# Spreading a recurrence's pieces further, moving inverses within SBUF, and reciprocal square roots by GpSimd's power

## The chip, the cores and the metric

One core of one Trainium2 chip. The metric is the device time of one execution in microseconds (us). A core has TensorE (PE, matrix products), VectorE (DVE), ScalarE (ACT), GpSimd (POOL) and SyncE (SP), which in this kernel issues all the transfers (DMAs). Each engine takes its instructions from its own queue in order; an instruction that waits holds all those behind it on its engine, and none on another.

## The reference

One layer of a streaming encoder over 4096 prompt tokens with 1024 features, and over 32 sample tokens that continue running streams with caches of their own. Group A is a short gated convolution, group B a gated delta rule with 4 heads of 128.

```python
h    = rmsnorm(x, ln_pre)
proj = h @ w_in     # columns: B_a | C_a | X_a | Z_a | qkv | Z_g | a_dec | b_beta
y_a  = b_a * conv3(c_a * x_a) * silu(z_a)
q, k, v = split(silu(conv4(qkv)));  q, k = l2norm(q), l2norm(k)
g    = -exp(a_log) * softplus(a_dec + dt_bias);  beta = sigmoid(b_beta)
S_t  = exp(g_t) (I - beta_t k_t k_t^T) S_{t-1} + beta_t k_t v_t^T;  o_t = q_t^T S_t / sqrt(dk)
y_g  = rmsnorm(o, gdn_norm_w) * silu(z_g)
y    = x + rmsnorm(concat(y_a, y_g) @ w_out, ln_post)
```

The reference evaluates the delta rule chunk by chunk: within a chunk a unit lower triangular matrix is inverted, from chunk to chunk the state S is handed on. The reciprocal square roots are those of the three norms.

## The kernel before

It runs in three stages: stage 1 (group B, and the transposed input for group A), group A, and the output products.

**Stage 1** takes the prompt in 16 blocks of 256 tokens, two chunks of 128 each; the sample's 32 tokens go with the first block. A block has eight steps (q, k, v and z, two column pairs each) of two projections, a projection being 24 products of 128x256 with weights in two float16 halves (`pj` in the profile, L74). After every projection stands a numbered slot, 16 to a block: pieces of other work are hung into the slots of their block or of the next (`at_slot`), and `run_slot` writes them out there. From block 1 on PE's order is exactly the written one: `Ordered` (T) ties each product or transpose to the one before it. The order on the other engines comes from a scheduler, which simulates the program and puts each instruction into its engine's queue by its simulated start.

The pieces of one block, in order:

- `xprep`: RMS-norm of the tokens of the next block (`xss`), with a reciprocal square root, and their transposition by DMAs; `gates` and `decays` for g and beta.
- `norm_qk` and `gram` (slots 7 to 12): normalisation and the products k k^T and q k^T (`gq` in the profile). The masked results M and `at` are kept, and the four 32x32 diagonal blocks of M of every chunk and head go through a DRAM buffer (`lad`) into the tile `la`, which holds the 32 blocks four times, 8 columns of the inverse for each copy. `rnorms` takes one square root (`r`, 128x16) for the q and k norms of the block.
- `subst`: the forward substitution, 31 steps of a multiplication and a subtraction on POOL (L551, L552), each depending on the one before. The result `lt` holds the inverses of the 32x32 blocks. It is written to DRAM (`ltd`, L555) and gathered from there by eight DMAs into `Tc` (L562), in pieces of 32 bytes.
- `merge` in five pieces: DVE transposes `Tc` into U (L583), then PE and DVE (`Rx`, L599) build the inverses of the whole chunks from the blocks, in the PSUM bank "m".
- `rec_a`, one for each chunk, in four pieces: transposed v (`rt`); k S and q S (`rk`, `rq`); U times the corrected v (`rv`), copied by ACT to `vn` (L652); and the new state (`rS`).
- `rec_b`, one for each chunk, in two pieces: the output products `at` times `vn` (`oo`), added to o by DVE, with the norm of o (`so`, 128x4, one reciprocal square root, then L682); and then the transposes of o (`om`), multiplied into `zg` by DVE (L688) and sent to DRAM by a DMA. Both pieces have their results in the PSUM bank "o", of which there is one buffer. So there is of "m".

`finish(p, s0)` hangs the merge and the recurrence of a block into slots 22 to 39 counted from the block's own first slot: that is into the second half of its own block and the first half of the next. `prep_a` prepares weights of group A besides, one in each of blocks 1 to 13 and two in 4, 7 and 10: loads (`xtw`), multiplications on DVE (L206) and POOL (L735, L741), and DMAs to `wad`.

`rsqrt` (L132) computes a reciprocal square root on DVE with eleven operations: a shift and a multiplication with an addition on the integers for a first value (L134, L135), and three rounds of Newton's method (L137 to L139).

**The transition.** After the last block, what is left in the slots (the rest of block 14, and block 15's merge and recurrence) is written out at once, the pools are closed, and group A begins (from here on the scheduler orders PE, too, and puts the rest among the first products of group A): `h_load` builds the operands `op` (for the first 512 tokens on DVE), and `winograd` makes seven products of half the size in place of eight (`pja`, `ga`).

**The output stage** multiplies by w_out (`pjo`, `go`, `ro`) and norms each half block (`norm_out`, one reciprocal square root, `oss`) before the sum is written.

Of the kernel before, what the change touches and what calls it, by code (L numbers as in the profile page):

```python
# [11 lines left out]
F32 = mybir.dt.float32  # L12
I32 = mybir.dt.int32
# [5 lines left out]
P = 128  # L19
# [30 lines left out]
def hybrid_kernel(  # L50
# [81 lines left out]
    def rsqrt(x, y, t):  # L132

        V.tensor_scalar(t.bitcast(I32), x.bitcast(I32), 1, None, ALU.logical_shift_right)  # L134
        V.tensor_scalar(y.bitcast(I32), t.bitcast(I32), -1, float(0x5F3759DF), ALU.mult, ALU.add)  # L135
        for _ in range(3):
            V.tensor_tensor(t, y, y, ALU.mult)  # L137
            V.scalar_tensor_tensor(t, t, -0.5, x, ALU.mult, ALU.mult)  # L138
            V.scalar_tensor_tensor(y, t, 1.5, y, ALU.add, ALU.mult)  # L139
# [113 lines left out]
    def xprep(b):  # L253
# [7 lines left out]
        ss = te([P, 3, 2], F32, "xss", 2, b["id"])[:m, :, :n // m]  # L261
# [12 lines left out]
        rsqrt(ss[:, 0], ss[:, 1], ss[:, 2])  # L274
# [229 lines left out]
    def rnorms(b):  # L504
# [3 lines left out]
        rt = te([P, 2, 2, NH], F32, "rt", 2, b["id"])[:C, :nch].rearrange("p c x h -> p (c x h)")  # L508
        sf = b["ss"].rearrange("p c x h -> p (c x h)")
        V.tensor_scalar(sf, sf, EPS, None, ALU.add)  # L510
        rsqrt(sf, rf, rt)
# [10 lines left out]
    def subst(b):  # L522
# [30 lines left out]
        b["subst_end"] = getattr(last, "ins", last)  # L553
        ltd = dp.tile([4, 32, 256], F32, tag="ltd", bufs=2, name=f"ltd{b['id']}")
# [13 lines left out]
    def merge(b):  # L568
# [11 lines left out]
        Tf = Tc.rearrange("p c h e -> p (c h) e")  # L580
        for q in range(nb):
            s = slice(32 * q, 32 * q + 32)
            V.transpose(Uf[s, :, s], Tf[s])  # L583
# [11 lines left out]
        for q in (0, 2):  # L595
            s0, s1 = slice(32 * q, 32 * q + 32), slice(32 * q + 32, 32 * q + 64)
            for c, h in ch:
                T.matmul(px[s1, c, h], M[c][s0, h, s1], Tc[s0, c, h], start=True, stop=True)
            V.tensor_tensor(X[s1], px[s1], bc(nb_[s1], 3, 32), ALU.mult)  # L599
# [63 lines left out]
    def rec_b(b, c):  # L663
# [5 lines left out]
        po = bank("o", [P, NH, P], f"o{nm}")[:C]  # L669
# [3 lines left out]
        so = tl([P, 3, NH], F32, "so", 2, nm)[:C]  # L673
# [6 lines left out]
        rsqrt(so[:, 0], f, so[:, 2])  # L680
# [143 lines left out]
    def finish(p, s0):  # L824
# [5 lines left out]
        if n == 1:  # L830
            for i, g in enumerate((ra[0], ra[0], mg, ra[0], ra[0], rb[0])):
                at_slot(s0 + 16 + i, next, g, None)
            at_slot(s0 + 24, ends, rb[0])
            at_slot(s0 + 24, out_state, p)
            return
        at_slot(s0 + 22, next, ra[0])
        at_slot(s0 + 23, next, ra[0])
        for i in range(5):
            at_slot(s0 + 24 + i, next, mg, None)
        at_slot(s0 + 29, next, ra[0])  # L840
        at_slot(s0 + 30, ends, ra[0])
        at_slot(s0 + 30, next, rb[0])
        at_slot(s0 + 28, next, ra[1])
        at_slot(s0 + 32, next, ra[1])
        at_slot(s0 + 34, next, ra[1])
        at_slot(s0 + 34, ends, rb[0])
        at_slot(s0 + 35, ends, ra[1])
        at_slot(s0 + 35, next, rb[1])
        at_slot(s0 + 39, ends, rb[1])
        if p["last"]:  # L850
            at_slot(s0 + 36, out_state, p)
# [83 lines left out]
    T.on = False  # L935
    early.close()
    for i in sorted(slots):
        run_slot(i)
    late.close()
# [3 lines left out]
    pl2 = ctx.enter_context(tc.tile_pool(name="pl2", bufs=1, side="right", reuse_waits="tile"))  # L943
# [32 lines left out]
    def winograd(lts, rhs, ps, c11, c12, c21, c22):  # L976
# [4 lines left out]
        for i, p in enumerate(ps):  # L981
            mm3(p, lts[i], rhs[i], True, True)
            if i == 0:
# [154 lines left out]
    rm = t3([P, KT], F32, "rm")  # L1138

# [102 lines left out]
    def norm_out(nm, tiles, iv, m, src, dst, E=(G, G), order=(0, 1)):  # L1242

        nt = len(tiles)
        ss = t3([P, 3, 2, 2], F32, "oss", 2, nm)[:m, :, :nt]
# [7 lines left out]
        s, f, w = ss[:, 1, :, 0], ss[:, 1, :, 1], ss[:, 2, :, 0]  # L1253
        V.tensor_tensor(s, ss[:, 0, :, 0], ss[:, 0, :, 1], ALU.add)
        V.tensor_scalar(s, s, 1.0 / D, EPS, ALU.mult, ALU.add)
        rsqrt(s, f, w)
# [34 lines left out]
    a_pairs(1, ops[1], 0)  # L1291
    for i in range(4, 8):
        operands(i)
# [66 lines left out]
```

## Time and profile before

| | |
|---|---|
| median of 3 runs | 2538.49 us (2527.29 to 2549.32) |
| profiled execution | 2536.03 us, its span 2534.2 us |
| busy: PE, DVE, POOL, ACT | 2178.5, 1697.0, 1168.1, 1003.4 us |
| share of the span | 86%, 67%, 46%, 40% |
| mean granted clock of TensorE | 0.928 |

Blocks 0 and 1 with the weights' preparation lie between 0 and 282 us of the span, blocks 2 to 15 between 282 and 1470, the transition between 1470 and 1536, group A from there to 2150, the output after that. In the rows, a time in brackets is idle time of that engine ahead of the instruction, with the instruction that ended it behind the arrow. An operation's tile is named without its number. A group of waits gives the sum, the count and the longest.

### The profile page before, as it was taken

What the parts mean: (1) busy time and instruction counts of PE and PEld (TensorE: products, weight loads), DVE (VectorE), ACT (ScalarE), POOL (GpSimd) and SP (SyncE); (2) the same over time, 40 slices, a digit from 0 to 9 for tenths busy, and PEclk for the clock granted to TensorE, in tenths of its full rate; (3) what the DMA queues carried; (4) which work ended last, traced back from release to release, by engine and by line L of the source; (5) the groups of instructions that cost most, each with busy time, mean ns of one, the idle gap of its engine ahead of it and who ended that gap; (6) DMA issues with size and microseconds to landing.
All of it is one profiled execution on the core that took longest, in us unless ns stands there. A gap on an engine that the chain in (4) does not pass through costs nothing. (4 is left out here: it accounts for less than half of the span.)

```text
span 2534.2 us, 48623 instructions
## 1 busy us (share of the span) xinstructions
PE 2178.5 (86%) x18626; PEld 1745.3 (69%) x18626; DVE 1697.0 (67%) x4666; ACT 1003.4 (40%) x2497; POOL 1168.1 (46%) x1581
## 2 busy tenths in 40 slices
PE   4666988699878987888889879999999999999998
PEld 3555776577767776777777768878888888544443
DVE  4885767676777677767865667556667466576772
ACT  4453555355545554555554422112221111333331
POOL 3524532544454445344642464175665442265552
PEclk9777988898999888989989889999999999999999
DMA  6343323423332433234422331521212103344331
GB/s 117 53 106 78 80 60 72 89 69 101 80 90 63 108 79 90 62 102 86 92 55 52 114 104 27 202 76 49 77 51 75 51 30 134 111 146 153 115 128 67
DMA packets 296914, 221.40 MB, mean 87 GB/s; under 512 B 166392, under 2 KB 236856, under 8 KB 296680
## 3 DMA queue, kind: packets, MB, share of 16 engines
q1 hardware_dynamic: 296680, 218.28, 31.4%
q8 instruction: 146, 2.39, 0.4%
q14 instruction: 88, 0.72, 0.1%
HBM read 127.84 MB, written 74.64 MB: 80 GB/s over the span
## 5 line engine op out<-in xcount | busy, mean ns | idle before, releaser
L74 PEld LDWEIGHTS <-w 128*128 128x128 f16 x6528 | 640.8, 103 | 126.0 <-POOL w L714 24.2
L74 PE MATMUL pj_c<-hhi,w 128*128 128x256 f16 x3072 | 583.3, 290 | 0.0
L74 PE MATMUL pj_c<-hlo,w 128*128 128x256 f16 x1536 | 445.4, 290 | 0.0
L74 PEld LDWEIGHTS <-w_a 128*128 128x128 f16 x2880 | 272.1, 99 | 62.2 <-issue 26.5
L547 POOL TENSOR_TENSOR la<-la,lt 128x1024 f32<-128x1024 f32 x16 | 37.8, 2361 | 581.7 <-DVE lt L542 536.7
L74 PEld LDWEIGHTS <-opm 128*128 128x128 f16 x1536 | 149.1, 98 | 189.3 <-issue 13.8
L552 POOL TENSOR_TENSOR lt<-lt 128x112 f32<-128x112 f32 (+29 forms) x496 | 237.5, 479 | 38.7
L551 POOL TENSOR_TENSOR lt<-la,lt 128x112 f32<-128x112 f32 (+29 forms) x496 | 219.0, 442 | 38.9
L436 DVE SCALAR_TENSOR_TENSOR qk<-u,cw,qk 128x256 f32<-128x256 f32 x384 | 208.4, 587 | 4.8 <-ACT qk L434 4.8
L74 PE MATMUL pja<-op,w_a 128*128 128x256 f16 x1536 | 193.8, 276 | 6.7 <-ACT d L984 2.7
L74 PE MATMUL pj_z<-hhi,w 128*128 128x256 f16 x1024 | 180.3, 275 | 0.0
L74 PE MATMUL ga<-op,w_a 128*128 128x256 f16 x1152 | 152.2, 279 | 14.6 <-DVE w L988 7.0
L1186 POOL TENSOR_TENSOR mab<-mab 128x1024 bf16<-128x1024 bf16 (+2 forms) x48 | 103.6, 2158 | 128.1 <-ACT mab L1184 125.7
L74 PE MATMUL pj_z<-hlo,w 128*128 128x256 f16 x512 | 140.5, 274 | 0.0
L74 PE MATMUL pjo<-w_o,opm 128*128 128x512 f16 x528 | 118.2, 379 | 3.8 <-DVE v13y L1261 2.0
L74 PE MATMUL ro<-w_o,opm 128*128 128x512 f16 x504 | 113.1, 379 | 4.3 <-DVE v7y L1261 2.3
L988 DVE TENSOR_TENSOR w<-pja,w 128x256 f32<-128x256 f32 x168 | 67.3, 420 | 73.7 <-PE pja L74 70.6
L74 PE MATMUL go<-w_o,opm 128*128 128x512 f16 x504 | 112.7, 379 | 3.9 <-DVE v19y L1261 2.0
L1003 ACT ACTIVATE op<-tsc 128x512 f16<-128x512 f32 x60 | 37.8, 630 | 192.9 <-POOL tsc L1009 113.0
L468 ACT ACTIVATE jk<-gt 128x128 bf16<-128x128 f32 x256 | 71.0, 278 | 100.8 <-PE gt L77 95.2
L988 DVE TENSOR_TENSOR w<-ga,w 128x256 f32<-128x256 f32 x121 | 51.0, 422 | 77.6 <-PE ga L74 69.8
L436 DVE SCALAR_TENSOR_TENSOR v<-u,cw,v 128x256 f32<-128x256 f32 x192 | 84.6, 477 | 9.0 <-ACT v L434 9.0
(697 smaller groups left out, 4664.0 us busy)
## 6 DMA issues: line engine op xcount, KB each, us to landing
xt<-in_x_prompt_dram SPq DMA_DIRECT2D x32, 512.0 KB
op<-hTd SPq DMA_DIRECT2D x32, 512.0 KB
mx<-mxd SPq DMA_DIRECT2D x16, 1024.0 KB
xtw<-in_w_in_dram SPq DMA_DIRECT2D x28, 512.0 KB
wad<-hl SPq DMA_DIRECT2D x56, 256.0 KB
gB<-gd SPq DMA_DIRECT2D x16, 516.0 KB
hTd<-hhi SPq DMA_DIRECT2D x16, 512.0 KB
hTd<-hlo SPq DMA_DIRECT2D x16, 512.0 KB
```

Of the source, the lines that this page charges most:

```text
L74: return self.queue(nc.tensor.matmul(*a, **k))
L436: V.scalar_tensor_tensor(d, u[:, i, j:j + n], cw[:, j, c0 + i:c0 + i + 1], d, ALU.mult, ALU.add)
L468: A.activation(jk[:C], tp[:C, h, :], AF.Square, accum_out=b["ss"][:, c, x, h:h + 1])
L547: E.tensor_tensor(la, la, bc(rl, 1, 32), ALU.mult)
L551: E.tensor_tensor(tm, bc(la[:, j, j + 1:32], 2, w), bc(lt[:, j, 0:w], 1, r), ALU.mult)
L552: last = E.tensor_tensor(lt[:, j + 1:32, 0:w], lt[:, j + 1:32, 0:w], tm, ALU.subtract)
L988: V.tensor_tensor(dst, p, src, ALU.add)
L1003: A.activation(f[:, q, 0, hf], t, AF.Copy)
L1186: G.tensor_tensor(ab[:, 0:m], ab[:, 0:m], ab[:, m:2 * m], ALU.add)
```

## The change

1. `rsqrt` is one operation of POOL, a power with the exponent -0.5 read from a constant tile; a scratch tile is gone, and others have two rows instead of three.
2. For the prompt, `subst` no longer goes through DRAM. DVE transposes `lt` in blocks of 32x32 into the front of `la` (L554 of the new code), and 16 DMAs, 32 rows of 256 bytes each, copy from SBUF to SBUF into `Tc`, whose elements are laid out in another order; the transposes into U (now L590) and the first products of the merge read it accordingly. The first four of the DMAs fill the first quarter of the partitions, and so on.
3. The first products of `rec_b` use bank "m" (`mo` for `oo`); "o" keeps the transposes alone.
4. The pieces of `finish` stand in other slots (table below); the state goes out at slot 40 instead of 36.
5. The last slots are not written out at once: one of them follows each second of the first products of group A, with PE's order still the written one, until none is left. The pools are closed after that.

| piece, two chunks | slots before | slots now |
|---|---|---|
| first chunk, rec_a | 22, 23, 29, 30 | 24, 25, 31, 33 |
| merge | 24 to 28 | 26 to 30 |
| second chunk, rec_a | 28, 32, 34, 35 | 30, 35, 37, 39 |
| first chunk, rec_b | 30, 34 | 33, 38 |
| second chunk, rec_b | 35, 39 | 39, 44 |
| sample: rec_a, merge, rec_a, rec_b | 16 and 17, 18, 19 and 20, 21 and 24 | 19 and 20, 23, 24 and 25, 25 and 30 |

```diff
-    def rsqrt(x, y, t):
-
-        V.tensor_scalar(t.bitcast(I32), x.bitcast(I32), 1, None, ALU.logical_shift_right)
-        V.tensor_scalar(y.bitcast(I32), t.bitcast(I32), -1, float(0x5F3759DF), ALU.mult, ALU.add)
-        for _ in range(3):
-            V.tensor_tensor(t, y, y, ALU.mult)
-            V.scalar_tensor_tensor(t, t, -0.5, x, ALU.mult, ALU.mult)
-            V.scalar_tensor_tensor(y, t, 1.5, y, ALU.add, ALU.mult)
+    mhalf = const([P, 16], F32, "mhalf")
+    V.memset(mhalf, -0.5)
+
+    def rsqrt(x, y):
+
+        G.tensor_tensor(y, x, mhalf[:x.shape[0], :x.shape[-1]], ALU.pow)
...
         b["subst_end"] = getattr(last, "ins", last)
+        if not b["s"]:
+
+            X = la.rearrange("p a b -> p (a b)")[:, 0:256].rearrange("p (q m e) -> p q m e", q=4, e=8)
+            V.transpose(X.rearrange("p q m e -> p e m q"), lt.rearrange("p a e -> p e a"))
+            Tc = b["Tc"] = tl([P, 4, 2, NH, 8], F32, "Tc", 1, b["id"])
+            for q in range(4):
+                for g in range(4):
+                    dma(Tc[32 * q:32 * q + 32, g].rearrange("p c h e -> p (c h e)"),
+                        X[32 * g:32 * g + 32, q].rearrange("p m e -> p (m e)"))
+            return
...
-        Tf = Tc.rearrange("p c h e -> p (c h) e")
+        Tf = Tc.rearrange("p g c h e -> p (c h) g e")
         for q in range(nb):
             s = slice(32 * q, 32 * q + 32)
-            V.transpose(Uf[s, :, s], Tf[s])
+            V.transpose(Uf[s, :, s].rearrange("p a (g e) -> p a g e", e=8), Tf[s])
...
             for c, h in ch:
-                T.matmul(px[s1, c, h], M[c][s0, h, s1], Tc[s0, c, h], start=True, stop=True)
+                T.matmul(px[s1, c, h].rearrange("p (g e) -> p g e", e=8), M[c][s0, h, s1], Tc[s0, :, c, h],
+                         start=True, stop=True)
...
-        po = bank("o", [P, NH, P], f"o{nm}")[:C]
+        po = bank("m", [P, NH, P], f"o{nm}")[:C]
...
         if n == 1:
-            for i, g in enumerate((ra[0], ra[0], mg, ra[0], ra[0], rb[0])):
-                at_slot(s0 + 16 + i, next, g, None)
...
+            for i, g in ((19, ra[0]), (20, ra[0]), (23, mg), (24, ra[0]), (25, ra[0]), (25, rb[0])):
+                at_slot(s0 + i, next, g, None)
+            at_slot(s0 + 30, ends, rb[0])
+            at_slot(s0 + 30, out_state, p)
             return
...
-        at_slot(s0 + 35, next, rb[1])
-        at_slot(s0 + 39, ends, rb[1])
+        for i, g in ((24, ra[0]), (25, ra[0]), (26, mg), (27, mg), (28, mg), (29, mg), (30, mg), (30, ra[1]),
+                     (31, ra[0]), (33, ra[0]), (33, rb[0]), (35, ra[1]), (37, ra[1]), (38, rb[0]),
+                     (39, ra[1]), (39, rb[1]), (44, rb[1])):
+            at_slot(s0 + i, next, g, None)
...
-    T.on = False
     early.close()
-    for i in sorted(slots):
-        run_slot(i)
-    late.close()
...
             mm3(p, lts[i], rhs[i], True, True)
+            if i % 2 and slots:
+                run_slot(min(slots))
...
     a_pairs(1, ops[1], 0)
+    while slots:
+        run_slot(min(slots))
+    T.on = False
+    late.close()
```

DVE's queue where block 8 is projected and block 7's inverse arrives. First before the change; `so6_1` and `o6_1` are the norm and the output of block 6's second chunk, `qk8` the convolution of block 8, `Tc7` the inverses of block 7.

```order
L681 TENSOR_TENSOR so6_1_9934<-so6_1_9934,sm6_8368 128x4
L682 TENSOR_TENSOR o6_1_9767<-o6_1_9767,so6_1_9934 128x512
L436 SCALAR_TENSOR_TENSOR qk8_9722<-u8_0_10003,cw_98,qk8_9722 128x256 x6
L429 COPY u8_8_10243<-hist7_8640 128x2x3
L688 SCALAR_TENSOR_TENSOR zg6_7586<-om6_1_10088,gwc_95,zg6_7586 128x4x128
L431 COPY hist8_9725<-u8_2_10075 128x6
L436 SCALAR_TENSOR_TENSOR qk8_9722<-u8_2_10075,cw_98,qk8_9722 128x256
L639 SCALAR_TENSOR_TENSOR R7_0_10046<-rk7_0_10095,sm7_9453,R7_0_10046 128x128 x4
L436 SCALAR_TENSOR_TENSOR qk8_9722<-u8_2_10075,cw_98,qk8_9722 128x256 x5
L471 TENSOR_TENSOR kd8_0_10124<-gt08_0_10115,E38_9602 128x512
L429 COPY u8_10_10389<-hist7_8640 128x2x3
L583 STREAM_TRANSPOSE U_144<-Tc7_9538 32x8x32 x4
```

And the same place of DVE's queue now; `la7` and `lt7` are block 7's tiles of the substitution, `mo6_1` the output products of block 6's second chunk.

```order
L554 STREAM_TRANSPOSE la7_9153<-lt7_9154 128x8x8x4
L434 SCALAR_TENSOR_TENSOR qk8_9415<-u8_2_9738,cw_98,qk8_9415 128x256
L680 TENSOR_TENSOR o6_1_9608<-o6_1_9608,mo6_1_9761 128x512
L434 SCALAR_TENSOR_TENSOR qk8_9415<-u8_2_9738,cw_98,qk8_9415 128x256 x2
L469 TENSOR_TENSOR kd8_0_9787<-gt08_0_9778,E38_9305 128x512
L434 SCALAR_TENSOR_TENSOR qk8_9415<-u8_2_9738,cw_98,qk8_9415 128x256 x2
L686 TENSOR_TENSOR so6_1_9767<-so6_1_9767,sm6_8096 128x4
L427 COPY u8_10_10054<-hist7_8367 128x2x3
L687 TENSOR_SCALAR so6_1_9767<-so6_1_9767 128x4
L590 STREAM_TRANSPOSE U_146<-Tc7_9231 32x8x32
L689 TENSOR_TENSOR so6_1_9767<-so6_1_9767,sm6_8096 128x4
L690 TENSOR_TENSOR o6_1_9608<-o6_1_9608,so6_1_9767 128x512
```

The transpose of the substitution's result is new, ahead of the add that reads `mo6_1`. The transposes into U stand apart (one of the four is in these rows), and between L687 and L689 there is one operation of DVE where eleven were between L679 and L681 before: the power is on POOL in that time.

POOL's queue inside the substitution of block 7, before, at the steps on 160 to 144 elements:

```order
L551 TENSOR_TENSOR lt7_9460<-la7_9459,lt7_9460 128x160
L552 TENSOR_TENSOR lt7_9460<-lt7_9460 128x160
L551 TENSOR_TENSOR lt7_9460<-la7_9459,lt7_9460 128x152
L552 TENSOR_TENSOR lt7_9460<-lt7_9460 128x152
L551 TENSOR_TENSOR lt7_9460<-la7_9459,lt7_9460 128x144
L552 TENSOR_TENSOR lt7_9460<-lt7_9460 128x144
```

And now; L137 is the power, `so6_0` the norm of block 6's first chunk.

```order
L548 TENSOR_TENSOR lt7_9154<-la7_9153,lt7_9154 128x160
L549 TENSOR_TENSOR lt7_9154<-lt7_9154 128x160
L548 TENSOR_TENSOR lt7_9154<-la7_9153,lt7_9154 128x152
L549 TENSOR_TENSOR lt7_9154<-lt7_9154 128x152
L137 TENSOR_TENSOR so6_0_9499<-so6_0_9499,mhalf_100 128x4
L548 TENSOR_TENSOR lt7_9154<-la7_9153,lt7_9154 128x144
L549 TENSOR_TENSOR lt7_9154<-lt7_9154 128x144
```

One power stands between two steps of the substitution here; that of block 9's tokens (`xss9`) stands further up, also inside it.

DVE's queue in the transition, now; `op0` is the operand of the first 512 tokens for group A (the put writes its second half), `R14_1` belongs to the recurrence of block 14, `d00` and `w31` to the first products of group A.

```order
L647 SCALAR_TENSOR_TENSOR R14_1_17381<-rk14_1_17899,sm14_16288,R14_1_17381 128x128 x4
L554 STREAM_TRANSPOSE la15_17212<-lt15_17213 128x8x8x4
L1000 TENSOR_TENSOR op0_17503<-w28_tsc_17508,op0_17503 128x512
L1000 TENSOR_TENSOR op0_17503<-tsc0_1_17527,op0_17503 128x512
L984 TENSOR_TENSOR w31_0_00_0_17816<-pja0_00_2_17820,w31_0_00_0_17816 128x256
L984 TENSOR_TENSOR d00_00_1_17817<-pja0_00_2_17820,d00_00_1_17817 128x256
L984 TENSOR_TENSOR w31_0_00_0_17816<-pja0_00_2_17820,w31_0_00_0_17816 128x256
L590 STREAM_TRANSPOSE U_146<-Tc15_17290 32x8x32 x2
```

Before, all puts of `op0` stood ahead of the first operation of DVE that waits for the end of block 15's substitution (the transposes into U); now two of them stand behind one.

## Rows read from the trace of the kernel before

**Rows 1.** Stretch; busy us of PE, PEld, DVE, ACT, POOL; PEclk, DMA, GB/s

```profile
282.00:1470.00 1188.00, 1008.09 (x9176) 873.75 (x9175) 837.10 (x2572) 619.71 (x1644) 538.97 (x1038) 0.90 0.33 83
1470.00:1536.00 66.00, 49.00 (x522) 39.37 (x521) 51.31 (x135) 15.73 (x49) 49.03 (x75) 0.84 0.25 78
1536.00:2150.00 614.00, 588.00 (x5418) 517.73 (x5416) 379.17 (x809) 119.29 (x244) 303.42 (x239) 0.99 0.23 79
2150.00:2535.00 385.00, 361.31 (x1749) 170.95 (x1746) 235.75 (x540) 118.05 (x260) 172.91 (x106) 0.99 0.36 119
```

**Rows 2.** PE's waits, 282 to 1470 us; sum, times, longest, us

```profile
PE om L77 <- DVE o L682: 49.1, 7, 17.6
PE oo L74 <- DVE zg L688: 44.0, 13, 4.6
PE m L74 <- DVE Rx L599: 33.4, 14, 5.5
PE rS L74 <- ACT vn L652: 20.1, 13, 2.3
PE m L74 <- DMA Tc<-ltd: 13.8, 16, 7.4
```

**Rows 3.** PE in time; start, us, engine line op out<-in, [idle before]

```profile
801.68 1.06 PE L74 MATMUL oo<-vn,at 128*128 128x128 f32 x8
...
823.99 2.08 PE L74 MATMUL oo<-vn,at 128*128 128x128 f32 x8 [2.88 <-DVE zg L688]
```

**Rows 4.** DVE's waits, 282 to 1470 us; sum, times, longest, us

```profile
DVE gu L333 <- ACT gex L329: 22.6, 13, 1.7
```

**Rows 5.** DVE's busy time of L137, L138 and L139, 282 to 1470 us

```profile
282.00:1470.00 1188.00, 32.43 (x165) 0.90 0.33 83
...
282.00:1470.00 1188.00, 39.23 (x165) 0.90 0.33 83
...
282.00:1470.00 1188.00, 36.21 (x165) 0.90 0.33 83
```

**Rows 6.** POOL in time

```profile
802.03 2.36 POOL L547 TENSOR_TENSOR la<-la,lt 128x1024 f32<-128x1024 f32 x1 [27.60 <-DVE lt L542]
...
836.96 3.63 POOL L735 TENSOR_TENSOR hl<-xtw,hl 128x512 f16<-128x512 f32 x3
840.53 0.31 POOL L543 MEMSET lt<- 128x256 f32 x1
840.80 1.33 POOL L741 TENSOR_TENSOR xtw<-xtw 128x512 f32<-128x512 f32 x1
```

**Rows 7.** SP's issues in time: an ordinary block, and one with two weights

```profile
837.02 0.33 SPq L555 DMA_DIRECT2D ltd<-lt  x1
...
838.75 4.36 SPq L562 DMA_DIRECT2D Tc<-ltd  x8
...
748.16 1.09 SPq L555 DMA_DIRECT2D ltd<-lt  x1
...
756.38 4.28 SPq L562 DMA_DIRECT2D Tc<-ltd  x8
```

**Rows 8.** Groups by line, 282 to 1470 us; busy, mean ns | idle

```profile
L583 DVE STREAM_TRANSPOSE U<-Tc 32x256 f32<-32x256 f32 x56 | 24.3, 435 | 12.0 <-DMA Tc<-ltd 11.1 <-issue 0.2
```

**Rows 9.** DVE in time, in a block with two weights

```profile
752.01 1.22 DVE L206 TENSOR_TENSOR xtw<-xtw,lnp 128x1024 f32<-128x1024 f32 x1 [8.96 <-DMA xtw<-in_w_in_dram]
```

**Rows 10.** PE's waits, 0 to 282 us

```profile
PE rvs L74 <- DVE Uss L574: 23.3, 1, 23.3
...
PE gcs L74 <- DVE g L352: 12.2, 1, 12.2
```

**Rows 11.** SP's issues in time, transition

```profile
1513.93 0.32 SPq L555 DMA_DIRECT2D ltd<-lt  x1
```

**Rows 12.** PE's waits, 2150 us to the end (the longest of six)

```profile
PE ro L74 <- DVE v7y L1261: 2.3, 1, 2.3
```

**Rows 13.** PE in time, the last Gram products of a block

```profile
791.76 1.46 PE L74 MATMUL gq<-qk 128*128 128x256 f32 x6
```

## What the change will do

> **What bounds the kernel now.** I read the busy time by stretch first [rows 1]. TensorE (PE) is the busiest engine in the three long stretches. Group A's products (1536 to 2150 us) and the output stage have little to give: 588 of 614 and 361 of 385 us are busy. The steady stage, blocks 2 to 15 of stage 1 (14 blocks, 282 to 1470 us, 85 us a block), has 1008 of 1188 busy: PE waits 180 us. VectorE (DVE) is busy 837, ACT 620 and GpSimd (POOL) 539, so none of them is a bound by its sum; each matters through what stands behind what in its queue.
>
> Next, PE's waits in that stage [rows 2]. Five account for 160 of the 180: the output transposes `om` behind DVE's multiplication of the last ones (49.1), the output products `oo` for bank "o" (44.0), the merge's first products for the inverses, named by DVE's `Rx` (33.4) and by the DMA `Tc` (13.8), and the state products `rS` behind ACT's copy `vn` (20.1). PE runs one fixed order, so each wait stops everything.
>
> Third, what a wait costs beyond itself [rows 3]. Eight `oo` products took 1.06 us after unbroken work and 2.08 us after a wait of 2.88 us: the granted clock had fallen to the lower of its two levels, 1.2 instead of 2.4 GHz. The granted clock averages 0.90 in the steady stage and 0.99 in group A's, which hardly waits. The 0.09 between them is 91 of the 1008 busy us at most; since part of that mean may fall in idle time, I count some 70.
>
> Last, the other queues: DVE's waits [rows 4], its square-root lines [rows 5], and the way of the inverses from POOL over SP to DVE [rows 6 to 8].
>
> **The change, part by part.**
>
> *Square roots.* Eleven DVE operations become one POOL power. In the steady stage nine of the eleven hold 32.4 + 39.2 + 36.2 = 107.9 us in 55 calls [rows 5], 0.22 us each; with the other two at that mean a call is 2.4 us and the stage's 55 calls are 132, four to a block: 9.4 us of DVE per block go. DVE is not the bound, so this buys earlier results, not time by itself. A power's duration is in no row. Below it is bounded by POOL's shortest row, a memset of 0.31 us; above by its operations on 128x512 and 128x1024, 1.33 and 2.36 us [rows 6]. Its shapes are 128x2 to 128x16, near the short end, so I take 0.5. Each call now goes from DVE to POOL and back. The nearest row is DVE's wait for a small ACT operation that it has just fed, 22.6 us in 13 times, 1.7 each [rows 4]. If all four turn-rounds of a block stop DVE, that is 7 us; if the order puts enough other work between, nothing. The order shows other DVE work in some and little in others, and it adds a stop at the transpose of `lt`. I take 4 us of new lateness per block, all of it passed to PE: **+56** (0 to +98). Two powers stand in POOL's queue inside the substitution and lengthen it by 1 us.
>
> *The way of the inverses.* Before, the substitution ended at 837.0, where POOL's next work starts, one write to DRAM was issued then, the eight gathers from 838.75 to 843.1 [rows 6, 7], and DVE's four transposes ran at about 847 to 849: 12 us. In a block that prepares two weights the gathers left eight us after the write [rows 7]. Now a DVE transpose of 128x256 comes first; by the four transposes of 32x256 (0.435 us each [rows 8]) it costs about 0.45 us. Then 16 SBUF copies at the eight gathers' pace, 0.55 us each, take 9, and landing about 2: 11 to 12 us to the last quarter, but the first is there after about 5, and each U transpose needs one quarter only. The trip through DRAM under load goes. The merge also starts two slots later, 2 × 5 us. `Tc` and `Rx`, 47 us, should fall to 10: **−37** (−47 to −10). SP issues seven more a block, some 3 us of its queue, behind which only loads with a block of time to spare stand.
>
> *Banks and slots.* With the first products in bank "m" the wait of 44.0 loses its cause: "m" is freed by the merge three slots before, and by the add of the first chunk six slots before the second: **−44**. The state products now come two projections after the copy's source, not one: the mean wait of 1.5 us (20.1 in 13) is well under the one slot, 85/16 = 5.3 us, that is put between: **−20**. Of `om`'s 49.1, three waits in the blocks that prepare two weights hold 41, the longest 17.6. Their cause is that DVE stands for weight loads (one stop is 8.96 us [rows 9]), and that stays; the second `om` comes five slots later than before, which absorbs part. Three such stops are 27; I keep 24 of the 41 and drop the other 8: **−25**. The 20 us of small waits stay.
>
> Steady waits: 180 − 44 − 20 − 25 − 37 + 56 = 110. The lower clock I scale with the waits: 70 × 70/180 = **−27** (0 to −36). The stage gives −70 − 27 = −97.
>
> *Start.* The sample's `rvs` waits 23.3 us for its inverse [rows 10] and now comes four slots later, 20 us: **−20** (0 to −23). Behind 12.2 us of waiting for the gates stand three square roots in DVE's queue: **−5**.
>
> *Transition to group A.* Before, the scheduler had laid the two last blocks' rests among group A's first products, with PE idle for 17 of 66 us [rows 1]. Now that order is the written one, with more products between two pieces, which could fill the 17. But DVE's order puts the transpose of block 15's `lt` ahead of the second operand's put, and that substitution ended at about 1513.9 [rows 11]. The stage's last projection ends near 1470 and some 20 us of products need no more than the first put: PE would stand from about 1490 until the transpose, 25 us in place of 17. I take **+8** (−17 to +25).
>
> *Output stage.* Six waits of about 2 us stand behind DVE's normalised output [rows 12]; eleven operations in that chain become one and a turn-round: **−5** (0 to −10).
>
> Sum: −97 − 20 − 5 + 8 − 5 = −119. On the span of 2534.2 this is 2415; what lies around the span adds 1.8 (2536.0 − 2534.2), and the median of the runs shown lies 2.5 above the profiled execution: 2419.5, say **2420 us**. With the bounds of the terms taken as independent, its own range is 2355 to 2480.
>
> **The rivals.**
>
> *DVE stops longer (18%).* For: the transpose of `lt`, four U transposes and four power results are waits in an in-order queue that before had only the waits for `la` and `Tc` there, and behind them stand the convolution and the adds that PE reads. Against: DVE has 9.4 us a block less to do. Five us more a block, 70 in all: 2490.
>
> *No new lateness (9%).* The planner's order hides every turn-round: the 56 go and 0.4 of them in clock, 78 in all: 2342.
>
> *A slow power (10%), the other side.* The powers stand in POOL's queue, and POOL's path is the longest of a block: from the last Gram products (793.2 [rows 13]) to the substitution's start 802.0 [rows 6] with the wait for `la` in it, 35 to its end, 12 to the last `Tc`; that is 8.8 + 35 + 12 = 56, and three powers lie on it: 56 + 3t. From slot 12 to slot 26 or 27 there are 14.5 slots of 78/16 = 4.9 us, and some 2 us of slack for the step-wise arrival: 73. Beyond t = 5.5 us each us costs 3 a block, 42 in the stage; the gain of 119 is spent at t = 8.3, and at t = 10 the time is 2420 + 190 = 2610. For: no row shows this operation, and it is not one that is done by a multiplication or an addition. Against: 256 to 2048 elements, and POOL does 131072 in 2.36 us.
>
> *A pause before each power (5%).* If POOL had to change its program whenever the kind of operation changes, a pause p would lie ahead of each power and add to t: by the chain above it bites from p = 5, and one us beyond that point costs 42: 2462. Against it: POOL goes from tensor operations to a memset (0.31 us) and back with no gap in the rows [rows 6]. By the Trainium skill, page "GPSIMD Engine Reference", section "Instruction dispatch", the first call of a freshly loaded kernel pays about 6 us without a visible instruction; no row here shows such a load, and paid once it would be nothing.
>
> *Nothing moves (3%).* The waits freed are replaced one for one: 2534.
>
> **How the numbers follow.** The forecast has 55%. The range goes from 2325, below the case without new lateness, to 2510, above the longer stops, and leaves out the slow power, the case where nothing moves and the tails, 0.18. One per cent, about what a measurement of this kernel can tell from no change, is 25 us: 2513 and 2564. Faster: the forecast, the longer stops, no lateness, and the pause, less 4% of tails: 0.83. Slower: the slow power, 0.10. The rest, 0.07.
>
> **What would show it.** Right: no wait of the first output products on DVE's `zg`; `rS` waits near nothing; the merge's first wait below 1 us a block; powers of 0.3 to 0.8 us; DVE 125 us less busy in the steady stage (132 less 6 for the new transposes); blocks of 77 to 79 us, and a granted clock above 0.92. Wrong: powers over 5 us on POOL; DVE's waits for `lt`, `Tc` and powers above 8 us a block together, with PE's waits for DVE as large as before; or PE standing over 30 us between the first group-A products.

## The result, and the profile after

The changed kernel takes 2476.94 us in the median of 4 runs (2475.45 to 2478.44), the kernel before 2537.63 in runs beside it: a ratio of 0.976, 95% interval 0.9727 to 0.9793. The forecast was 2420, with a range of 2325 to 2510: the direction was right, the gain is half of what the sum gave, 61 in place of 119 us.

Busy time by stretch in the changed kernel (columns as in [rows 1]): block 1, the steady stage, transition and group A, output.

```profile
189.00:273.00 84.00, 68.71 (x647) 58.23 (x646) 49.32 (x158) 39.45 (x108) 32.82 (x70) 0.90 0.29 66
273.00:1402.00 1129.00, 982.58 (x9169) 858.84 (x9167) 765.65 (x1986) 604.70 (x1652) 616.42 (x1093) 0.93 0.33 85
1402.00:2097.00 695.00, 627.82 (x5877) 548.96 (x5876) 417.24 (x884) 132.72 (x285) 353.30 (x317) 0.97 0.21 74
2097.00:2476.00 379.00, 369.28 (x1830) 178.95 (x1827) 202.63 (x356) 120.12 (x268) 212.25 (x124) 0.99 0.38 126
```

Against [rows 1] the steady stage is 59 us shorter (1188 to 1129), PE's waits in it 33 fewer (180 to 146), its granted clock 0.93 for 0.90. DVE is 71 us less busy there, not 125. Transition and group A are longer, 695 us for 66 + 614 = 680.

What PE waits for in the steady stage of the changed kernel (sum, times, longest, us), to be held against [rows 2]:

```profile
PE m L74 <- DVE Rx L607: 56.5, 13, 7.4
PE om L77 <- DVE o L690: 20.9, 4, 6.5
PE rq L74 <- ACT R L640: 20.2, 9, 2.7
PE rv L74 <- DVE R L647: 14.0, 5, 4.7
PE m L74 <- ACT U L613: 11.4, 14, 1.6
PE rS L74 <- ACT vn L660: 11.3, 5, 8.3
PE m L74 <- DMA wad<-hl: 4.6, 1, 4.6
```

The wait of the output products is gone and that of the transposes is down from 49.1 to 20.9. The merge waits 57 for `Rx` in place of 47 for `Rx` and `Tc`, and `rq` and `rv` wait 34; before, `rv` waited 1.4 and `rq` never.

The powers, by tile (duration in ns, least, median and most; then first and last start, shapes):

```profile
L137 POOL TENSOR_TENSOR so<-so,mhalf x32: 999/1008/1025, 289.1 to 1543.0; 128x4 f32<-128x4 f32 x32
L137 POOL TENSOR_TENSOR oss<-oss,mhalf x17: 558/3897/3902, 2139.0 to 2469.1; 128x2 f32<-128x2 f32 x15, 128x1 f32<-128x1 f32 x2
L137 POOL TENSOR_TENSOR xss<-xss,mhalf x16: 695/696/717, 21.2 to 1258.8; 128x2 f32<-128x2 f32 x16
L137 POOL TENSOR_TENSOR r<-ss,mhalf x16: 2898/2899/2958, 169.7 to 1388.0; 128x16 f32<-128x16 f32 x16
```

A power takes 0.70, 1.01 and 2.90 us on 2, 4 and 16 columns: not one price of 0.5, but some 0.16 us a column on top of 0.4.

### The profile page after: what moved, and what is told of

It reads as the page before. It is cut to its first block, busy times and chain, and to the rows that moved or that the text cites. A ratio compares the mean times of both kernels' runs of the same rounds, so it can differ in the third digit from the quotient of the medians.

```text
span 2475.8 us, 48038 instructions
## 1 busy us (share of the span) xinstructions
PE 2152.9 (87%) x18626; PEld 1729.3 (70%) x18626; DVE 1569.7 (63%) x3748; ACT 986.8 (40%) x2497; POOL 1293.8 (52%) x1666
## 5 line engine op out<-in xcount | busy, mean ns | idle before, releaser
L74 PE MATMUL pj_c<-hhi,w 128*128 128x256 f16 x3072 | 576.6, 288 | 2.4 <-ACT u L428 2.2
L548 POOL TENSOR_TENSOR lt<-la,lt 128x112 f32<-128x112 f32 (+29 forms) x496 | 213.2, 430 | 37.5
L434 DVE SCALAR_TENSOR_TENSOR qk<-u,cw,qk 128x256 f32<-128x256 f32 x384 | 219.4, 611 | 13.5 <-ACT qk L432 13.4
L74 PE MATMUL pja<-op,w_a 128*128 128x256 f16 x1536 | 194.3, 277 | 20.2 <-DVE op L1000 5.0
L137 POOL TENSOR_TENSOR r<-ss,mhalf 128x16 f32<-128x16 f32 x16 | 46.4, 2903 | 225.9 <-DVE ss L507 225.9
L137 POOL TENSOR_TENSOR oss<-oss,mhalf 128x2 f32<-128x2 f32 (+1 forms) x17 | 50.0, 2942 | 114.7 <-DVE oss L1249 114.7
L435 ACT ACTIVATE qk<-qk 128x512 f32<-128x512 f32 x64 | 40.4, 631 | 142.4 <-DVE qk L434 142.4
```

Source lines behind the costliest of these rows:

```text
L74: return self.queue(nc.tensor.matmul(*a, **k))
L137: G.tensor_tensor(y, x, mhalf[:x.shape[0], :x.shape[-1]], ALU.pow)
L434: V.scalar_tensor_tensor(d, u[:, i, j:j + n], cw[:, j, c0 + i:c0 + i + 1], d, ALU.mult, ALU.add)
L435: queued("silu", lambda: A.activation(dst, dst, AF.Silu))
L548: E.tensor_tensor(tm, bc(la[:, j, j + 1:32], 2, w), bc(lt[:, j, 0:w], 1, r), ALU.mult)
```

## The experiments

Ratios are to the kernel before, run on the same chip in the same series. The steady stage runs from the start of block 2 to the end of the last projection, "rest" from there to the end of the span; both, and PE's waits in the steady stage, are of the profiled execution.

| kernel | ratio, 95% interval | block 1 starts | block 1 | steady | PE waits there | rest |
|---|---|---|---|---|---|---|
| before | 1 | 184.1 | 98.2 | 1188.0 | 179.8 | 1063.9 |
| changed | 0.976 (0.9727 to 0.9793) | 189.0 | 84.0 | 1129.0 | 146.5 | 1073.8 |
| u1_roots | 1.0068 (1.0049 to 1.0087) | 184.1 | 82.7 | 1198.8 | 213.7 | 1100.3 |
| u2_way | 0.9891 (0.9864 to 0.9918) | 189.0 | 83.8 | 1164.8 | 178.1 | 1082.6 |
| u3_bank | 0.9771 (0.9736 to 0.9806) | 189.2 | 84.5 | 1126.6 | 146.2 | 1077.1 |
| u4_slots | 1.0198 (1.0175 to 1.022) | 188.7 | 98.5 | 1232.0 | 237.8 | 1079.6 |
| u5_tail | 0.964 (0.9617 to 0.9663) | 190.3 | 83.9 | 1134.7 | 143.9 | 1044.2 |
| r_only | 0.977 (0.9743 to 0.9797) | 185.9 | 85.3 | 1134.3 | 145.0 | 1073.0 |
| later1 | 0.9883 (0.9855 to 0.991) | 190.2 | 84.8 | 1161.3 | 168.6 | 1073.1 |
| p_roots | 1.0094 (1.0061 to 1.0127) | 189.3 | 99.3 | 1235.2 | 209.4 | 1048.4 |
| p_slots | 0.99 (0.988 to 0.9921) | 185.3 | 82.5 | 1184.9 | 205.7 | 1070.2 |
| px_both | 0.9773 (0.9759 to 0.9788) | 190.7 | 85.9 | 1131.4 | 147.4 | 1073.9 |
| px_both_tail | 0.964 (0.9624 to 0.9657) | 188.3 | 84.5 | 1134.4 | 140.4 | 1043.7 |
| tail_free | 0.9623 (0.9601 to 0.9645) | 188.5 | 83.1 | 1128.3 | 142.2 | 1040.2 |

One hundredth of the ratio is 25 us. The four series ran on several chips, and the kernel before took 2537.63 to 2547.15 us in them; so kernels of different series are compared by their ratios, and the changed kernel's interval is 8 us wide to either side. The scheduler plans the queues of the engines other than PE anew for each kernel: what a run shows is an edit together with its new plan.

### Each part undone in the changed kernel

**Roots back on VectorE** (u1_roots):

```diff
-        rsqrt(so[:, 0], f)
+        rsqrt_v(so[:, 0], f, so[:, 2])
```

`rsqrt_v` is the root of the kernel before; the calls for `xss`, `r` and `oss` are changed in the same way.

> The changed kernel with all reciprocal square roots back on VectorE (eleven operations), the other four parts as changed. Theory A (the queue of VectorE and its load make the merge's first sums late; the powers relieve it): VectorE gets 9.4 us a block of work back, part of it in front of the merge, so the time rises by 2 to 4 us a block: 2505 to 2535 us. Theory B (the powers themselves are the delay: 0.7 + 1.0 + 2.9 us of them lie on GpSimd's chain from the Gram products to the inverse): 3 to 4.6 us a block come back and the 56.5 us of waits for Rx fall by most: 2415 to 2440 us. If both cancel: within 10 us of 2477.

Measured 1.0068: 3.1 hundredths, 78 us, above the changed kernel, and above the kernel before. Theory B falls, and A's bound of 2535 was too low (2555 on the scale of the expectations, where the changed kernel stands at 2477). The profiled executions, of two series, lie 90 us apart: 70 in the steady stage and 26 after it, less 6 before it. PE's waits in the steady stage of this kernel:

```profile
PE om L77 <- DVE o L693: 103.9, 12, 17.7
PE m L74 <- DVE Rx L610: 74.6, 14, 9.6
```

With eleven operations in the norm of o on DVE, the transposes `om` wait 104 us where they wait 21 with the power, and `Rx` 75 for 57. Other waits shrink: the sum of PE's waits rises by 67.

**The old way of the inverses** (u2_way):

```diff
-        if not b["s"]:
-            V.transpose(X.rearrange("p q m e -> p e m q"), lt.rearrange("p a e -> p e a"))
...
+        dma(ltd.rearrange("g l f -> (g l) f"), lt.rearrange("p a b -> p (a b)"))
```

> The changed kernel with the old way of the inverses (one write to DRAM, eight gathers). By the prediction's term the new way was worth 37 us and its clock share: 2515 to 2530 us. Theory A (VectorE stands at the transpose of lt, 22.8 us in all, and the 16 issues of 10.8 us on SyncE are no quicker than write and gathers): the new way is worth nothing by itself: 2460 to 2485 us.

Measured 0.9891, 1.3 hundredths or 33 us slower than the changed kernel (2510 on the scale of the expectations, 5 below the first of them); the steady stage is 36 us longer. The merge's waits, among those of PE in its steady stage:

```profile
PE m L74 <- DVE Rx L596: 93.2, 14, 10.0
...
PE m L74 <- DMA Tc<-ltd: 7.1, 17, 1.2
```

The way within SBUF takes 93.2 + 7.1 down to 56.5: 44 us of waiting, 32 in the sum of PE's waits. In the changed kernel it is worth about what its term said, and theory A, by which it would be worth nothing, is out. The trip through DRAM is not the whole of it, though: among DVE's own waits in the steady stage of this kernel the second longest is

```profile
DVE so L678 <- POOL so L137: 50.3, 16, 6.5
```

against 10.8 in the changed kernel: in this kernel's plan DVE also stands longer for the powers. That the new way has its worth only beside the powers is likely, but no run varies just that. The kernels with the roots on DVE and the new slots are u1_roots, with the new way, bank and transition, and p_slots below, without these three: the steady stage is 1198.8 us with them and 1184.9 without.

**The output products in bank "o"** (u3_bank):

```diff
-        po = bank("m", [P, NH, P], f"o{nm}")[:C]
+        po = bank("o", [P, NH, P], f"o{nm}")[:C]
```

> The changed kernel with the first output products back in bank o. The products of the second chunk stand one slot behind the transposes of the first again, as before, those of the first chunk five slots behind. By the prediction's term (44 us and its clock share): 2520 to 2540 us. Rival (the merge's lateness swallows it): 2477 to 2490 us.

Measured 0.9771, the interval over that of the changed kernel: nothing to be seen. PE's waits in its steady stage:

```profile
PE m L74 <- DVE Rx L607: 57.5, 13, 7.7
...
PE oo L74 <- DVE zg L696: 14.4, 13, 1.7
...
PE rq L74 <- ACT R L640: 7.1, 8, 1.7
```

The wait for the bank is back with 14.4 us, and `rq`, two slots behind, waits 13 less (20.2 to 7.1). The sum of PE's waits is 146.2 as against 146.5. What PE does not wait for at one place it waits for at the next.

**The old slots** (u4_slots; the table of slots as before):

> The changed kernel with the old numbers of the slots. The merge comes two slots (10 us) earlier. By the prediction's terms (20 for rS, 25 for om, some of the 37, 20 for the sample, clock): 2540 to 2560 us. Theories A and B both have the inverse late by 4 us a block already, so that 10 us more fall on the merge in each of 14 blocks: 2580 to 2620 us. If slots were worth nothing: 2477.

Measured 1.0198, 4.4 hundredths or 111 us slower than the changed kernel (2588 on the scale of the expectations): as theories A and B had it, and some 30 above the upper end by the prediction's terms. PE's waits in its steady stage:

```profile
PE m L74 <- DMA Tc<-la: 141.2, 28, 8.6
PE om L77 <- DVE o L690: 76.6, 14, 16.7
```

With powers in POOL's queue and the merge two slots earlier, the inverses themselves come 10 us a block too late. Block 1 is 98.5 long again, for 84.0, and the sample's `rvs` waits 16.4 in it: the slots there, the sample's above all, are worth 14.5 us.

**The old transition** (u5_tail; last slots written out at once, before group A):

> The changed kernel with the old transition: the last slots written out at once, the scheduler ordering TensorE there. From the last projection to the end the changed kernel takes 1073.8 us, the kernel before 1063.9. If the written order with the stop at block 15's transpose is what costs them, as the prediction's term of +8 has it: 8 to 12 us faster, about 2465 to 2470. If the ten us have another cause (the output stage, the clock), or the old order would now meet a later substitution and cost the same: within 5 us of the changed kernel.

Measured 0.964: 1.2 hundredths, 30 us, faster than the changed kernel, all of it in the rest (1073.8 to 1044.2). The expectation had the sign and a third of the size.

### What the transition loses

**The pieces written as in the changed kernel, TensorE's order free** (tail_free):

```diff
+    T.on = False
     early.close()
```

> The changed kernel with the last slots still written among group A's first products, but TensorE's order free from there on, as before. If the fixed order of TensorE is what costs the 30 us that the old transition gives back: 2445 to 2460 us. If it is the place in which the pieces are written (and so VectorE's order): within 8 us of 2477.

Measured 0.9623, within noise of the old transition and the fastest kernel of all: 2448.69 us beside 2542.39 for the kernel before. The rest takes 1040.2. So with PE's order free the place in which the pieces are written costs nothing that could be seen; the fixed order of PE, with the plan that the other engines get by it, costs the 34 us. The stretch behind the last projection by busy time, first in the changed kernel:

```profile
1402.00:1500.00 98.00, 63.34 (x651) 51.47 (x650) 61.27 (x126) 20.86 (x58) 71.38 (x95) 0.81 0.15 51
```

and then with the order free:

```profile
1400.00:1480.00 80.00, 64.96 (x708) 53.94 (x707) 61.74 (x130) 19.69 (x56) 63.89 (x88) 0.89 0.19 63
```

PE stands 35 of 98 us at a granted clock of 0.81 there, and 15 of 80 at 0.89 here, where it gets through more products (708 for 651) in less time. One of the stops of the changed kernel, first DVE in time (start, duration, idle before in brackets):

```profile
1439.64 1.11 DVE L647 SCALAR_TENSOR_TENSOR R<-rk,sm,R 128x128 f32<-128x128 f32 x4
1443.72 0.68 DVE L554 STREAM_TRANSPOSE la<-lt 128x256 f32<-128x256 f32 x1 [2.97 <-POOL lt L549]
1444.29 0.65 DVE L1000 TENSOR_TENSOR op<-w_tsc,op 128x512 f16<-128x512 f32 x1
```

and PE in time:

```profile
1444.99 1.22 PE L74 MATMUL pja<-op,w_a 128*128 128x256 f16 x5 [4.98 <-DVE op L1000]
```

DVE stands for the end of block 15's substitution, the put of the operand `op` stands behind it, and PE's product waits 4.98 us for the put. This is the stop that the prediction drew from DVE's order; but it is 5 us of the 35. The others are sums and puts of group A (`ga` for `w`, 11.0 us in three waits, the longest 6.1; `ga` for `op`, 5.8) that DVE or ACT has not done when the written order asks for them.

### What the merge's wait is

**One kind of roots back on VectorE** (r_only: `r`, 128x16, the 2.9 us on the way from the Gram products to the substitution):

> The changed kernel with one of its four kinds of roots, that of the q and k norms (128x16, 2.9 us on GpSimd, on the way from the Gram products to the substitution), back on VectorE: eleven operations of about 0.17 us, 1.9 us, no turn-round. If the length of the chain on GpSimd is what makes the merge late: 1 to 2 us a block come back, 2450 to 2465 us. If VectorE's load is what counts: a quarter of the 78 us that all four kinds cost, 2490 to 2500 us.

Measured 0.977, nothing. The steady stage is 5 us longer, the start 3 us shorter. Neither theory's interval holds. That what is won on POOL's chain is spent on DVE would explain it, but is not shown.

**All pieces one slot later** (later1: 25 to 45 for 24 to 44):

> The changed kernel with all pieces of finish for two chunks one slot later (25 to 45 in place of 24 to 44). If the 56.5 us of waits of the merge for Rx are only its lateness against the written order, 5 us more of other products cover nearly all of them: 40 to 70 us faster, 2410 to 2440. If the wait follows VectorE's queue, which is full behind the substitution's end, it moves to the next piece and the time stays within 15 us of 2477.

Measured 0.9883, 31 us slower: further off than either theory said. PE's waits in its steady stage:

```profile
PE m L74 <- DVE Rx L607: 68.6, 14, 7.4
PE rv L74 <- DVE R L647: 46.9, 7, 12.1
PE ggate L74 <- DVE kd L469: 14.4, 6, 2.9
```

With 5 us more for the inverses the merge waits twelve us more, not less, and `rv` waits 46.9 behind DVE's `R` where it waited 14.0. So the merge's wait in the changed kernel is no lateness of the inverses.

**The first piece of the merge in another order** (px_both). In the changed kernel, PE in time:

```profile
1298.14 0.69 PE L74 MATMUL m<-Tc,M 32*32 32x32 f32 x16
1302.35 1.06 PE L74 MATMUL m<-Tc,M 32*32 32x32 f32 x16 [3.52 <-DVE Rx L607]
```

and DVE in time at the same place:

```profile
1300.60 0.88 DVE L434 SCALAR_TENSOR_TENSOR v<-u,cw,v 128x256 f32<-128x256 f32 x2
1301.40 0.17 DVE L322 TENSOR_TENSOR gz<-gz,ug 128x16 f32<-128x16 f32 x1
...
1301.88 0.42 DVE L607 TENSOR_TENSOR Rx<-m,sm 32x256 f32<-32x256 f32 x1
```

The first half of the products is done at 1298.8; `Rx` stands in DVE's queue behind a convolution and the gates of the next block, until 1301.88, with no idle time; and the second half, which does not read `Rx`, waits for it, because `Rx` reads the bank that it writes. The edit takes that wait away by order:

```diff
                 T.matmul(px[s1, c, h].rearrange("p (g e) -> p g e", e=8), M[c][s0, h, s1], Tc[s0, :, c, h],
                          start=True, stop=True)
+        for q in (0, 2):
+            s1 = slice(32 * q + 32, 32 * q + 64)
             V.tensor_tensor(X[s1], px[s1], bc(nb_[s1], 3, 32), ALU.mult)
```

> The changed kernel with one edit in the merge's first piece: the products for the third quarter are written before VectorE's multiplication Rx of the first quarter, and not after it. In the changed kernel these products, which read only Tc and M, wait for that multiplication, because it reads the same bank. Theory (the 56.5 us of waits for Rx are this place in VectorE's queue, and no lateness of the inverses): the waits for Rx fall from 56.5 to below 15 us, 40 to 70 us faster, 2405 to 2440 us. Rival (the inverse itself is late): the wait moves to the DMA Tc or to the second piece and the time stays within 15 us of 2477.

Measured 0.9773: nothing. The waits for `Rx` fell to 15.3, near what the theory had, but of PE's waits in its steady stage these are the first and the fourth:

```profile
PE m L74 <- ACT U L615: 51.9, 14, 4.9
...
PE m L74 <- DVE Rx L609: 15.3, 7, 3.8
```

The second piece waits 51.9 where it waited 11.4. What the rival forecast came, the wait at the second piece and the time unchanged; its cause, a late inverse, did not: `Tc` is waited for 5.7 us in all. The sum is 147.4, as in the changed kernel.

**The same in both pieces, with the old transition** (px_both_tail):

> The same edit in the first and the second piece of the merge, and the old transition to group A. If the two gains add up (24 us of the transition and 40 to 70 of the first edit, some 5 to 10 of the second): 2375 to 2415 us. If the merge's edit gives nothing: about 2453.

Measured 0.964: the transition's gain and none from the merge. With the second piece cleared as well, PE's two longest waits in the steady stage are

```profile
PE gt L77 <- DVE at L489: 47.8, 13, 5.0
PE m L74 <- DMA Tc<-la: 24.9, 10, 4.2
```

The next transposes in PE's order (`gt`, of q and k) wait 47.8 for DVE's `at`, where they waited 3.3. (With both pieces cleared, the inverses themselves are late at times: `Tc` is waited for 24.9.) Twice the wait was taken from one place, and each time some 50 us, 3.5 a block, stood at the next piece that needs DVE, directly or by ACT.

### Two parts alone on the kernel before

**The powers alone** (p_roots; slots, bank, way and transition as before):

> The kernel before with the powers alone. If the powers are worth by themselves what their removal costs (78 us): about 2460 us. If they lengthen GpSimd's chain by 4.6 us a block and the old slots leave no room for it, as the run with the old slots suggests: 0 to 60 us slower, 2540 to 2600. By the prediction's term alone (4 us of new lateness a block and its clock): 2615.

Measured 1.0094, 24 us slower. The profiled execution is 38 longer: the steady stage 47, the start 5, the rest 15 shorter. PE's waits in the steady stage:

```profile
PE m L74 <- DMA Tc<-ltd: 83.1, 107, 6.3
PE om L77 <- DVE o L679: 42.7, 7, 13.0
```

In the old slots the inverses come later: `Tc` is waited for 83.1 for 13.8. Two things lengthen the way to them, the powers on POOL's chain and DVE's stops for `so`, 43.7 us in this stage; the run doesn't tell them apart. Busy time in the stage, columns as above:

```profile
289.00:1524.00 1235.00, 1025.61 (x9175) 883.65 (x9174) 720.25 (x1971) 618.97 (x1644) 620.40 (x1092) 0.89 0.33 80
```

DVE is 117 us less busy than before here, near the forecast, and not 71 as in the changed kernel.

**The slots alone** (p_slots; all else as before):

> The kernel before with the new numbers of the slots alone. By the prediction's terms for the slots (rS 20, om 25, the sample 20, part of the merge's 47, and the clock): 60 to 100 us faster, 2440 to 2480. By the pair that is left when each is undone (slots undone: 111 slower, roots undone: 78 slower, both together gaining only 60 to 90): slots alone are 20 us slower to 10 us faster than before, 2525 to 2560.

Measured 0.99, 25 us faster (2512 on the scale of the expectations), a little beyond the second expectation and far from the first. The profiled execution, the slowest of the four, is 11 us shorter than that of the kernel before: block 1 gave 15.7 (98.2 to 82.5), the steady stage 3 (1188.0 to 1184.9); the start and the rest took 7 back. Where the other 14 of the 25 lie is not shown. PE's waits in the steady stage:

```profile
PE om L77 <- DVE o L682: 103.3, 13, 19.2
PE m L74 <- DVE Rx L599: 66.3, 14, 8.4
```

The bank's 44 and `rS`'s 20 are gone here, too, and `om` waits 103.3 in place of 49.1, `Rx` and `Tc` 68 in place of 47.

## Why the prediction was right, and where not

**Direction and place**: right. By place the changed kernel has −59 in the steady stage for −97, −9 ahead of it for −25, +15 in the transition and group A for +8, −5 in the output for −5. The granted clock rose with fewer waits (0.90 to 0.93), and PE's busy time in the steady stage fell by 25.5, near the forecast 27; but that was scaled from waits falling by 70, and they fell by 33, so the agreement is luck.

**The sum of the waits**, 180 to 146 where it had 110. The three waits to be freed gave 81 of 89. New waits at `rq`, `rv` and a few others came to some 38 where 56 were put. The step that failed most is the merge's: its wait rose by 9 us where the sum had it fall by 37.

**Banks and slots**, −44 − 20 − 25: the waits fell much as the steps said (`oo` to nothing, `rS` to 11.3, `om` to 20.9), but that a freed wait is gained time was a step that failed. The bank undone costs nothing (u3_bank), and the slots alone, which free `oo` and `rS` as well, give 3 us of the steady stage in the profiled execution. Undone in the whole (u4_slots) the slots cost 111, by late inverses (141.2) and `om` (76.6) and not by `rS` (2.4). Moreover the fall of `om` is not the work of the slots, which alone bring it to 103; the powers take it from 104 to 21.

**Square roots**, +56: wrong in sign for the change as a whole. I had written that relief of DVE buys no time by itself and priced the turn-rounds only. With the other parts in place they are worth 78 us, by `om` most visibly; in the old slots and alone they cost 24. DVE's stops for powers are small in the changed kernel, 10.8 us for `so` and 2.3 for `r` in the whole stage, and that at the transpose of `lt` is 22.8, in seven blocks. The turn-rounds that the term priced do exist in other orders: 43.7 us for `so` in p_roots, 50.3 in u2_way. The power's price was missed by size: 0.7 to 2.9 us where 0.5 was taken, some 4.6 a block on the way from the Gram products to the inverses.

**The way of the inverses**, −37: undone, the new way costs about that (33, u2_way). But the term had the wait end at 10, and it stands at 57; without the new way it stands at 100. The two slots by which the merge starts later do take away the wait for the inverses' arrival, which is 141.2 us of PE's waits in the old slots (u4_slots) and none in the changed kernel. What the step missed is the other wait: later1 and px_both show that the 57 are the place of `Rx` in DVE's queue, which later slots don't shorten.

**DVE's new lateness**: it is this that ate the gain, in the changed kernel mostly not through the turn-rounds. PE's waits stand at 146, and three edits (u3_bank, px_both, px_both_tail) moved them and left the sum at 140 to 147. Shown is that the merge's wait, where it is taken away, comes up again where PE next needs DVE, directly or by ACT, as late as the next block's transposes of q and k. Open is which loop through DVE, ACT and POOL sets the 3.5 us a block; no run settles it. One part can be read off: operations that DVE has in both kernels became longer, so that it lost 71 us of work and not 125 (last section). The powers alone don't do that: with them alone it lost 117 (p_roots).

**Start**, −20 and −5: the later slots gave 14 in block 1 (the wait of 23.3 [rows 10] is gone, and `rqs` waits 13.3 in its place). Before block 1 it went 5 us the other way, and the wait for the gates that was to shrink from 12.2 is 15.6: kernels with the powers begin it at 188 to 191, those without at 184 to 185, and the one that has all but `r` at 185.9.

**Transition**, +8: +15 came, inside the bounds of the term, but the mechanism named is the smaller part. The stop behind the transpose of block 15's `lt` is there, with 5 us; PE's written order costs 34 by tail_free, against the same kernel with the order free. I had looked for the one wait on the substitution and not at the sums and puts of group A, which in the kernel before PE could go around.

**Output**, −5: 384.2 to 378.8, and the six waits [rows 12] are gone.

**The rivals**: the time lies between the forecast and "DVE stops longer" (2490), nearer to the latter; DVE is indeed what PE waits for, though the stops that this rival names, at `lt` (22.8), `U` (8.5) and the powers (13.1), are 3.2 us a block and not 5 on top of 4. A slow power was far from its point of 5.5 us.

**Luck**: of the prediction's signs of being right two came, no wait of the first output products and a clock above 0.92. The others did not: `rS` waits 11.3, the merge's first wait is 4 us a block, powers take up to 2.9, DVE lost 71 us, and a block of the steady stage takes 80.6. The time lies in the range since errors went opposite ways: the roots were priced as a loss and are a gain with the new slots, the freed waits were priced as a gain and came back elsewhere.

## What to carry to other kernels

A wait on the bounding engine is a term of a sum only if the engine that it names would not be met again, as late, at the next piece: before adding up waits, ask which engine they have in common and whether the change makes that engine's queue shorter. Two parts that give little or lose alone (later slots, 25 us faster, and the roots moved to another engine, 24 slower) can each be worth much in the whole (111 and 78 us when undone); undoing each in the whole, and doing each alone, tells it. An engine's order that is fixed by hand should be tried free where two stages mix: here that gave 34 us at the transition. Whether the fixed order pays within the steady stage no run tells.

## What the runs showed of the hardware

The time of a power on GpSimd goes with its columns and varies little otherwise in stage 1: 0.70, 1.01, 2.90 us for 2, 4, 16. In the output stage twelve of the fifteen powers on 2 columns took 3.90. POOL in time, at one such place and at a later one:

```profile
2406.20 3.90 POOL L137 TENSOR_TENSOR oss<-oss,mhalf 128x2 f32<-128x2 f32 x1 [5.95 <-DVE oss L1249]
...
2427.59 0.71 POOL L137 TENSOR_TENSOR oss<-oss,mhalf 128x2 f32<-128x2 f32 x1 [9.49 <-DVE oss L1249]
```

and DVE in time at the first:

```profile
2406.29 3.24 DVE L1196 SCALAR_TENSOR_TENSOR mx<-mx,rm,msc 128x256 f32<-128x256 f32 x8
2410.13 0.16 DVE L1251 TENSOR_TENSOR oss<-oss,iv 128x2 f32<-128x2 f32 x1 [0.61 <-POOL oss L137]
```

The slow one lies over eight operations of DVE with two operands in SBUF, 3.24 us without a gap, and ends 0.57 after them; the one at 2427.59, with nothing of that kind beside it, takes 0.71. All twelve of 3.90 us lie over the same group of eight, and none of the three of 0.71 does. The reverse is there as well: beside a POOL operation on 128x512 a DVE operation on 128x4 took 1.24 us,

```profile
1214.48 1.27 POOL L751 TENSOR_TENSOR xtw<-xtw,xtw 128x512 f32<-128x512 f32 x1
1214.53 1.24 DVE L686 TENSOR_TENSOR so<-so,sm 128x4 f32<-128x4 f32 x1
```

and a block later, in a block with no weights to prepare, 0.16:

```profile
1291.66 0.16 DVE L686 TENSOR_TENSOR so<-so,sm 128x4 f32<-128x4 f32 x1
```

The Trainium skill, page "GPSIMD Engine Reference", section "Key points", says that GpSimd shares its SBUF interfaces with VectorE, with contention for VectorE's instructions with two SBUF inputs; these rows agree. That this is why DVE's common operations became longer is argued, not shown. More work on POOL is not enough for it: p_roots has POOL busy as long as the changed kernel (620 and 616 us) and DVE 117 us less busy than before. What is left as a reading is that the two engines' operations meet at other places in the changed kernel's order.
